# An MLP whose four engines follow one computed order, with seven-product groups in all but four places

## The chip, the cores and the metric

The kernel runs on one core of a Trainium2 chip. The metric is the device time of one execution in microseconds (us). Before the change three runs gave 2020.44 us in the median (2019.13 to 2021.89).

Five engines matter here: TensorE (PE in the profile; PEld is its weight load), VectorE (DVE), ScalarE (ACT), GpSimd (POOL, almost unused) and SyncE (SP), which issues the DMA transfers that bring weights from HBM. Each engine runs its own list of instructions in a fixed order and waits on semaphores.

## What is computed

A two-layer decoder trunk on 256 tokens of width 2048, in float32. Each layer is a mixer, a norm, an MLP and a norm; the change is in the MLP only:

```python
def sq_relu_mlp(x, w1, w2):
    return jnp.square(jax.nn.relu(x @ w1)) @ w2          # 2048 -> 8192 -> 2048

for layer in range(DEPTH):                                # DEPTH = 2
    mix = short_conv_mixer(...) if layer < N_A else mla_mixer(...)
    h = layer_norm(ALPHA * h + mix, ln_g[layer, 0], ln_b[layer, 0])
    h = layer_norm(ALPHA * h + sq_relu_mlp(h, mlp_w1[layer], mlp_w2[layer]), ln_g[layer, 1], ln_b[layer, 1])
```

## The kernel before

Every float32 weight is split into a high part `hi`, rounded to the format float32r by ScalarE (`split`, L144), and a rest `lo`, formed by VectorE (L145). A product x·w is then three matmuls, hi·w_hi, hi·w_lo, lo·w_hi (`dot`, L307 to L309), or two of 512 and 256 columns where the activations' two parts stand side by side (`mm_like`, L242 and L246). Weights stream through six raw buffers (`raw`, 512 KB each) into a ring of eight `hi`/`lo` pairs (`whl`, WA = 8).

The MLP has 64 chunks of 128 hidden units. The first eight come out of the fused norm; each of the other 56, a step "m" of the list `steps`, takes 16 matmuls of 512 columns and 16 of 256 into the bank `ps_m`, is moved out by ScalarE and VectorE (`whole`, L348 and L349) and squared. The second matrix is applied in 56 groups per layer: 28 pairs of chunks (j) by two halves (b) of the output. A group is a two-by-two block product. A "plain" group does it with eight products, into banks 1 to 4 of the accumulators `sum`. A "fast" group does it with seven (the Strassen-Winograd form) into seven banks: VectorE must first form four 512-wide differences of the weights (L193), and two more splits are due, `hi_t`/`lo_t` of 1024 and `t4` of 512. The last eight chunks go through `down` (`ps_d`) at the end.

Ten groups of a layer are plain (`PLAIN`, L39): j = 0 and 1 of both halves, and j = 4, 8, ..., 24 of the second half, where a run of that half begins. Since both halves share the banks, at each change of half ScalarE copies every bank to SBUF (`spill`, L595) and loads the other half's sum into it (`seed`, L599).

What runs when: `plan` lists groups and chunks in turn; the code emits each step's operations in that order, loads and splits running ahead by the ring; the language's scheduler then fixes each engine's list.

Of the kernel before, what the change touches and what calls it, by code (L numbers as in the profile page):

```python
# [15 lines left out]
P = 128  # L16
W = 256 + 2
# [19 lines left out]
SLOTS = 10  # L37
FIRST = ((0, 2, 4, 8), (0, 4, 8))
PLAIN = ((0, 1), (0, 1, *range(4, KEPT, 4)))  # L39
# [9 lines left out]
def trunk(ctx: ExitStack, tc: tile.TileContext, xT, vecs, w_in, w_out, w_kv, w_q, w_uk, w_uv,  # L49
          w_qn, w_qp, w_o, w1, w2, w2f, cosT, sinT, mask, ident, gb, out):  # L50
    nc = tc.nc
    PS = bass.MemoryType.PSUM
    const = ctx.enter_context(tc.tile_pool(name="const", bufs=1))
# [27 lines left out]
    def plan():  # L81

        nxt, b, steps, m, count = [0, 0], 0, [], QC, 0
# [10 lines left out]
        return steps + [("m", i) for i in range(m, FF // P)]  # L94

    steps = plan()

    def mlp_stream(l):
        out = halves(w1[l, :QC])
        for s in steps:  # L100
            if s[0] == "m":
                out += halves(w1[l, s[1]])
            else:
                out.append(("plain" if s[3] else "fast", w2f[l, s[1], s[2], 0], w2f[l, s[1], s[2], 1]))
        return out + halves(w2[l])

    stream += mlp_stream(0) + halves(w_kv) + halves(w_q)
# [3 lines left out]
    size = {"unit": 1, "plain": 2, "fast": 3}  # L111
# [27 lines left out]
    state = {"made": 0, "next": 0}  # L139
    ready = {}  # L140

    def split(hi, lo, src):

        nc.scalar.copy(hi, src)  # L144
        nc.vector.tensor_tensor(lo, src, hi.bitcast(F32), ALU.subtract)  # L145
# [7 lines left out]
    def load(i, raw, cuts):  # L153

        hi, lo = ready[i] = parts(i)
        for b0, b1 in zip(cuts, cuts[1:]):
            at, cols = slice(b0, b1), slice(P * b0, P * b1)
            nc.sync.dma_start(raw[:, cols], stream[i][1][:, cols])
# [4 lines left out]
    def load_raw(i, src):  # L163
        raw = raws.tile([P, 1024], F32, tag="raw", name=f"raw{i}")
        nc.sync.dma_start(raw, src)
        return raw

    def prepare(i):
# [15 lines left out]
        b11, b22, b21, b12 = r1[:, :BW], r1[:, BW:], r2[:, :BW], r2[:, BW:]  # L184
        out = {}
        if kind == "plain":
            out["11"], out["22"] = finished(r1, 1)
            yield
            out["21"], out["12"] = finished(r2, 2)
            ready[i] = out  # L190
            yield
            return
        minus = lambda o, x, y: nc.vector.tensor_tensor(o, x, y, ALU.subtract)  # L193
        out["11"], out["22"] = finished(r1, 1)
        minus(b11, b12, b11)
        minus(b12, b12, b22)
        minus(b22, b22, b11)
        yield
        out["T1"], out["T2"] = finished(r1, "t")
        minus(b11, b21, b22)  # L200
        yield
        out["21"], out["T3"] = finished(r2, 2)
        f = state["fast"].tile([P, 2, BW], F32R, tag="t4", name=f"t4_{i}", bufs=1)
        split(f[:, 0, :], f[:, 1, :], b11)
        out["T4"] = [f[:, 0, :], f[:, 1, :]]
# [3 lines left out]
    sequence, i = [], 2 * GROUP  # L209
    while i < len(stream):  # L210
        if [k for k, *_ in stream[i:i + 3]] == ["unit", "unit", "fast"]:
            sequence += [i + 2, i, i + 1, i + 2, i + 2]
            i += 3
        else:
            sequence += [i] * size[stream[i][0]]
            i += 1
# [12 lines left out]
    def take(n=2, ahead=None):  # L229
# [4 lines left out]
        make_up_to(max(mine, start[i] - 2 * GROUP + (WA if ahead is None else ahead)))  # L234
# [5 lines left out]
    def high(ps, w, blk, x, first):  # L240

        nc.tensor.matmul(ps, w[blk // 8][0][:, blk % 8, :], x, start=first, stop=False)  # L242

    def low(ps, w, blk, x, last):

        nc.tensor.matmul(ps[:, :T], w[blk // 8][1][:, blk % 8, :], x[:, :T], start=False, stop=last)  # L246
# [18 lines left out]
    def mm_k1(ps, w, blk, x, first, last):  # L265

        hi, lo = (t[:, blk % 8, :] for t in w[blk // 8])
        nc.tensor.matmul(ps[:, :T], lo, x[:, :T], start=first, stop=False)
        nc.tensor.matmul(ps[:, :T], hi, x[:, T:], start=False, stop=False)
        nc.tensor.matmul(ps[:, :T], hi, x[:, :T], start=False, stop=last)  # L270
# [6 lines left out]
    def mm_wide(wps, x, k0=0, k1=NC):  # L277

        for k in range(k0, k1):
            for w, ps in wps:  # L280
                hi, lo = (t[:, k % 8, :] for t in w[k // 8])
                nc.tensor.matmul(ps[:, :W], hi, x[k][:, :W], start=k == 0, stop=False)  # L282
                nc.tensor.matmul(ps[:, :W], lo, x[k][:, :W], start=False, stop=False)
                nc.tensor.matmul(ps[:, :W], hi, x[k][:, W:], start=False, stop=k == NC - 1)
# [20 lines left out]
    def dot(ps, w, x, first, last, goes_on=False):  # L305

        nc.tensor.matmul(ps, x[0], w[0], start=first, stop=False, skip_group_check=goes_on)  # L307
        nc.tensor.matmul(ps, x[0], w[1], start=False, stop=False, skip_group_check=goes_on)  # L308
        nc.tensor.matmul(ps, x[1], w[0], start=False, stop=last, skip_group_check=goes_on)  # L309
# [35 lines left out]
    def whole(ps, out):  # L345

        t = tmp.tile([P, T], F32, tag="evac", name="t")
        nc.scalar.copy(t, ps[:, T:])  # L348
        nc.vector.tensor_tensor(out, ps[:, :T], t, ALU.add)  # L349

    def put_split(dst, src):

        nc.scalar.copy(dst[:, :T], src)
# [787 lines left out]
```

## Time and profile before

| | |
|---|---|
| median of three runs | 2020.44 us |
| the profiled execution | 2019.17 us |
| its span, first to last instruction | 2017.4 us |
| groups and chunks of layer 1 | 412.78 to 1003.33 us |
| the same of layer 2 | 1363.19 to 1962.77 us |
| mean granted TensorE clock | 0.998 |

The two MLP stretches run from the first matmul into `sum` to the first into `ps_d`; together they are 59% of the span. In the views, a row of the timeline is start, duration, engine, line, operation, tiles and shape, with the idle time before it and what ended that in square brackets. A row of the groups gives count, busy time, mean duration in ns, then idle time and its releasers. A row of the windows gives for each engine the busy time in that stretch.

### The profile page before, as it was taken

How to read it: one execution, taken by the hardware profiler on the slowest of the kernel's cores; microseconds unless marked ns; L12 is line 12 of the kernel's file. 1: busy time of each engine (PE TensorE's matmuls, PEld its weight loads, DVE VectorE, ACT ScalarE, POOL GpSimd, SP SyncE). 2: the span in 40 equal slices, each digit the busy share in tenths (PEclk: the TensorE clock that was granted, in tenths of full speed). 3: DMA queues.
4: the chain of work that ended last, by engine and by line, in shares of the span. 5: the costliest groups of instructions: out<-in, count | busy, mean ns of one | idle time of the engine just before them, and what ended most of it. 6: DMA issues, size and time to landing. Idle time of an engine off the chain costs nothing.

```text
span 2017.4 us, 29774 instructions
## 1 busy us (share of the span) xinstructions
PE 1994.7 (99%) x11088; PEld 1737.5 (86%) x11088; DVE 1715.3 (85%) x2575; ACT 1381.1 (68%) x2071; POOL 2.3 (0%) x21
## 2 busy tenths in 40 slices
PE   9999999999999999999999999999999999999997
PEld 8888888988888888888889998898888888888886
DVE  7667677799999989999979878779999999898996
ACT  6444445587887788878756655568778788787871
POOL 0000000000000000000000000000000000000000
PEclk9999999999999999999999999999999999999999
DMA  9655556465666666666655534654666566565672
GB/s 321 205 188 189 189 188 193 149 184 186 194 209 188 211 206 188 211 187 219 228 176 165 162 119 136 195 176 151 206 197 210 176 209 202 180 219 184 209 236 99
DMA packets 108002, 385.31 MB, mean 191 GB/s; under 512 B 11984, under 2 KB 13392, under 8 KB 107856
## 3 DMA queue, kind: packets, MB, share of 16 engines
q1 hardware_dynamic: 107712, 383.13, 59.5%
q8 instruction: 87, 1.43, 0.3%
q14 instruction: 59, 0.48, 0.1%
q10 hardware_dynamic: 144, 0.26, 0.0%
HBM read 381.25 MB, written 2.10 MB: 190 GB/s over the span
## 4 chain that ended last, share of the span: by engine, by line
PE 82%; DVE 9%; ACT 4%; issue 2%; DMA 2%; DVEq 0%; ACTq 0%; SPq 0%
PE ps_m L242 16%; PE ps_u L242 13%; PE ps_m L246 8%; PE ps_u L246 7%; PE sum L307 7%; PE sum L308 7%; PE sum L309 7%; DVE lo L145 3%; DVE raw L193 2%; PE ps_d L309 1%; PE ps_d L308 1%; PE ps_d L307 1%; DMA raw<-in_w_dram 1%; ACT hi L144 1%; PE ps_w L282 1%
## 5 line engine op out<-in xcount | busy, mean ns | idle before, releaser
L145 DVE TENSOR_TENSOR lo<-raw,hi 128x1024 fp32r<-128x1024 f32 x712 | 856.3, 1219 | 126.5 <-ACT hi L144 49.3
L144 ACT CAST hi<-raw 128x1024 fp32r<-128x1024 f32 x712 | 735.4, 1052 | 273.5 <-PE ps_u L242 158.1
L242 PE MATMUL ps_m<-xhl,hi 128*128 128x512 f32 x1792 | 449.3, 391 | 2.3 <-DVE sf L349 2.1
L242 PEld LDWEIGHTS ps_m<-xhl,hi 128*128 128x128 f32 x1792 | 328.4, 188 | 68.2 <-DVE sf L349 3.9
L246 PEld LDWEIGHTS ps_m<-xhl,lo 128*128 128x128 f32 x1792 | 245.2, 190 | 17.9
L246 PE MATMUL ps_m<-xhl,lo 128*128 128x256 f32 x1792 | 250.8, 282 | 0.0
L307 PE MATMUL sum<-hi,hc 128*128 128x512 f32 x512 | 202.0, 395 | 4.8 <-ACT sum L599 4.8
L308 PE MATMUL sum<-lo,hc 128*128 128x512 f32 x512 | 200.4, 391 | 0.0
L193 DVE TENSOR_TENSOR raw<-raw,raw 128x512 f32<-128x512 f32 x276 | 189.0, 685 | 1.3
L309 PE MATMUL sum<-hi,ha 128*128 128x512 f32 x448 | 173.9, 390 | 0.0
L242 PE MATMUL ps_u<-xhl_a,hi 128*128 128x512 f32 x720 | 171.9, 391 | 0.0
L145 DVE TENSOR_TENSOR lo_t<-raw,hi_t 128x1024 fp32r<-128x1024 f32 x92 | 112.6, 1224 | 63.4 <-ACT hi_t L144 63.4
L242 PEld LDWEIGHTS ps_u<-xhl_a,hi 128*128 128x128 f32 x720 | 132.4, 188 | 25.7
L595 ACT COPY sums<-sum 128x512 f32<-128x512 f32 x204 | 118.4, 587 | 32.6 <-PE sum L309 31.9
L144 ACT CAST hi_t<-raw 128x1024 fp32r<-128x1024 f32 x92 | 96.6, 1050 | 56.1 <-DVE raw L193 55.5
L307 PEld LDWEIGHTS sum<-hi,hc 128*128 128x128 f32 x512 | 96.4, 188 | 27.7 <-ACT sum L599 10.2
L599 ACT COPY sum<-sums 128x512 f32<-128x512 f32 x186 | 110.9, 596 | 1.3
L308 PEld LDWEIGHTS sum<-lo,hc 128*128 128x128 f32 x512 | 96.5, 188 | 16.2
L348 ACT COPY t<-ps_m 128x256 f32<-128x256 f32 x112 | 41.7, 372 | 89.1 <-PE ps_m L246 89.1
L309 PEld LDWEIGHTS sum<-hi,ha 128*128 128x128 f32 x448 | 84.2, 188 | 17.6
L246 PEld LDWEIGHTS ps_u<-xhl_a,lo 128*128 128x128 f32 x720 | 92.3, 191 | 3.5
L246 PE MATMUL ps_u<-xhl_a,lo 128*128 128x256 f32 x720 | 93.4, 283 | 0.0
(240 smaller groups left out, 3273.9 us busy)
## 6 DMA issues: line engine op xcount, KB each, us to landing
raw<-in_w_dram SPq DMA_DIRECT2D x288, 512.0 KB, 4.4
raw<-in_w2f_dram SPq DMA_DIRECT2D x224, 512.0 KB, 4.1
raw<-in_w_in_dram SPq DMA_DIRECT2D x90, 512.0 KB, 4.3
raw<-in_w_out_dram SPq DMA_DIRECT2D x32, 512.0 KB, 4.0
raw<-in_w_o_dram SPq DMA_DIRECT2D x32, 512.0 KB, 3.7
raw<-in_w_kv_dram SPq DMA_DIRECT2D x10, 512.0 KB, 4.0
raw<-in_w_q_dram SPq DMA_DIRECT2D x8, 512.0 KB, 3.8
raw<-in_w_uk_dram SPq DMA_DIRECT2D x8, 512.0 KB, 4.4
```

The costliest lines, as they stand in the source:

```text
L144: nc.scalar.copy(hi, src)
L145: nc.vector.tensor_tensor(lo, src, hi.bitcast(F32), ALU.subtract)
L193: minus = lambda o, x, y: nc.vector.tensor_tensor(o, x, y, ALU.subtract)
L242: nc.tensor.matmul(ps, w[blk // 8][0][:, blk % 8, :], x, start=first, stop=False)
L246: nc.tensor.matmul(ps[:, :T], w[blk // 8][1][:, blk % 8, :], x[:, :T], start=False, stop=last)
L282: nc.tensor.matmul(ps[:, :W], hi, x[k][:, :W], start=k == 0, stop=False)
L307: nc.tensor.matmul(ps, x[0], w[0], start=first, stop=False, skip_group_check=goes_on)
L308: nc.tensor.matmul(ps, x[0], w[1], start=False, stop=False, skip_group_check=goes_on)
L309: nc.tensor.matmul(ps, x[1], w[0], start=False, stop=last, skip_group_check=goes_on)
L348: nc.scalar.copy(t, ps[:, T:])
L595: nc.scalar.copy(self.slot(self.live.pop(p)), self.bank[p])
L599: nc.scalar.copy(self.bank[p], self.at(key))
```

## The change

Three things change. First, `PLAIN` becomes 2: only j = 0 and 1 of each half are plain, so 52 groups of a layer are fast instead of 46. Second, the loop over `steps` in `mlp` is replaced by a list of all operations of the stage (class `Work`): each has its engine (T, A, V for TensorE, ScalarE, VectorE; S for a load), a length worked out from its columns, what it depends on, and a function that issues it. `times` gives every VectorE and ScalarE operation a latest start by which TensorE would not wait; `arrange` plays the engines against each other from these lengths, always taking the ready operation with the earliest such time; `issue` emits all in the order of their starts, and `keep_in_program_order` holds every engine, and SP's queue of loads, to it. The first four groups (`ALONE`) are loaded as before, ahead of the stage. Third, small things go along: an eleventh slot for spilled sums, T4 before T3 within a fast group, `prepare` of the next norm as operations of the list, the mask loaded in the attention part instead of at the start, and the weights of `down` requested after all loads of the list (`stops`). Since all operations go through a wrapper, they stand under L70 in lists of the changed kernel.

```diff
-SLOTS = 10
-PLAIN = ((0, 1), (0, 1, *range(4, KEPT, 4)))
+SLOTS = 11
+SPARE = 2
+ALONE = 4
+LEAD = 9000
+PLAIN = 2
...
+            def call(*args, **named):
+                ins = op(*args, **named)
+                kept = state["kept"]
+                if kept is None:
+                    return ins
+                if self not in kept:
+                    kept.add(self)
+                    return ins
+                return tc.keep_in_program_order(ins)
...
-            run = [(b, j, j in PLAIN[b]) for j in range(nxt[b], end)]
-            for i, (b, j, plain) in enumerate(run):
-                steps.append(("group", b, j, plain, i == 0, i == len(run) - 1))
-                if count >= 3 and m < FF // P:
-                    steps.append(("m", m))
-                    m += 1
-                count += 1
+            groups += [(b, j, j < PLAIN, j == end - 1) for j in range(nxt[b], end)]
...
+    def mlp_stream(l):
+        return halves(w1[l, :QC]) + [("plain", w2f[l, b, j, 0], w2f[l, b, j, 1]) for b, j, *_ in groups[:ALONE]]
...
+        stops.append(len(stream))
+        return halves(w2[l])
...
-        if [k for k, *_ in stream[i:i + 3]] == ["unit", "unit", "fast"]:
-            sequence += [i + 2, i, i + 1, i + 2, i + 2]
...
+            if stops and i >= stops[0]:
+                return
...
+        LATER = {"A": 140, "V": 125, "T": 210}
...
+            late, t = [0.0] * n, 0.0
+            for i, op in enumerate(self.ops):
+                if op[0] == "T":
+                    late[i] = t
+                    t += op[1]
+            for i in reversed(order):
+                engine, cost, _, _, early = self.ops[i]
+                if engine in "AV":
+                    late[i] = min([late[u] - (cost + self.LATER[engine] if ends else 0) for u, ends in self.users[i]],
+                                  default=t) - early
+            return late
...
+                    begun[i] = max(now, queue)
+                    queue = begun[i] + 100
+                    pipe = max(pipe, begun[i] + 1700) + 1550
+                    heapq.heappush(events, (pipe + 1000, i))
+                for e in "TAV":
+                    while free[e] <= now:
+                        if e == "T":
+                            if not turn or turn[0] not in able:
+                                break
+                            i = turn.pop(0)
+                        elif ready[e]:
+                            i = heapq.heappop(ready[e])[1]
+                        else:
+                            break
+                        begun[i], free[e] = now, now + ops[i][1]
+                        heapq.heappush(events, (free[e], -1))
+                        heapq.heappush(events, (free[e] + self.LATER[e], i))
+                        settle(i, False)
...
+            order = self.arrange(freed)
+            self.room = [None] * RAW
+            state["kept"] = set()
+            for i in order:
+                if self.ops[i][0] == "S" and self.room[self.places[i]] is None:
+                    self.room[self.places[i]] = raws.tile([P, 1024], F32, tag="raw", name=f"w{i}")
+                self.ops[i][2]()
+            state["kept"] = None
...
+        spans = {"A": lambda n: 0.82 * n + 110, "V": lambda n: n / 0.96 + 68}
...
+            ends.append(work.add("T", count * (columns + 32) / 2.4, run, known(deps), ends[-1:]))
...
+            c = add("A", 1024, lambda: scalar.copy(both()[0], raw()), load, *deps)
+            return both, c, add("V", 1024, lambda: less(both()[1], raw(), both()[0].bitcast(F32)), c)
...
+                first = ring_ops(loads[0])
+                x1 = add("V", BW, lambda: less(b11(), b12(), b11()), first[2], loads[1])
+                x3 = add("V", BW, lambda: less(b12(), b12(), b22()), x1)
+                x2 = add("V", BW, lambda: less(b22(), b22(), b11()), x3)
+                mid, end = ring_ops(loads[0], x2), ring_ops(loads[1], x3)
+                x4 = add("V", BW, lambda: less(b11(), b21(), b22()), mid[2])
...
+                x = add("A", BW, fourth, x4, fourths[-1])
+                l4 = add("V", BW, lambda: less(box["f"][:, 1, :], b11(), box["f"][:, 0, :].bitcast(F32)), x)
...
+                x = add("A", 512, lambda: sums.spill(p), banked[p], behind=back[-SPARE:-SPARE + 1 or None])
...
+                x = add("A", 512, lambda: sums.seed(p, key), x)
...
+        for i in range(ALONE):
+            group_ops(i)
+        made, loads = chunk_ops(QC)
+        work.loads += loads
+        entries += [c for _, c, _ in made]
+        for m, i in enumerate(range(ALONE, len(groups)), QC + 1):
+            made, loads = chunk_ops(m)
+            more, others = group_ops(i)
+            work.loads += [*others, *loads]
+            entries += [more[0][1], made[0][1], more[1][1], made[1][1], more[2][1]]
...
+                work.ops[e][3].append((frees[entries[n - WA]], True))
+                if not isinstance(entries[n - 1], tuple):
+                    work.ops[e][3].append((entries[n - 1], False))
+        work.issue(freed)
+        stops.pop(0)
```

VectorE in layer 1, before: the end of the fast group (0, 5) of half 0 (tiles `raw165`), the plain group (1, 4) of half 1 (`raw168`), and the start of the next fast group. `lo166` and `lo167` are the splits of a chunk, `sf` is a chunk being moved out.

```order
L193 TENSOR_TENSOR raw165_0_4762<-raw165_0_4762 128x512 [waits DVE_49]
L349 TENSOR_TENSOR sf_4818<-ps_m_4785,t_4819 128x256 [waits Activation_49]
L145 TENSOR_TENSOR lo165_t_4823<-raw165_0_4762,hi165_t_4822 128x1024 [waits Activation_49]
L145 TENSOR_TENSOR lo165_2_4828<-raw165_1_4764,hi165_2_4827 128x1024 [waits Activation_49]
L193 TENSOR_TENSOR raw165_0_4762<-raw165_1_4764,raw165_0_4762 128x512 [waits DVE_49]
L145 TENSOR_TENSOR lo166_4859<-raw166_4856,hi166_4858 128x1024 [waits DMAHW3_49,PE_49,Activation_49]
L145 TENSOR_TENSOR lo167_4865<-raw167_4862,hi167_4864 128x1024 [waits DMAHW4_49,PE_49,Activation_49]
L145 TENSOR_TENSOR t4_165_4831<-raw165_0_4762,t4_165_4831 128x512 [waits PE_49,Activation_49]
L145 TENSOR_TENSOR lo168_1_4873<-raw168_0_4868,hi168_1_4872 128x1024 [waits DMAHW5_49]
L349 TENSOR_TENSOR sf_4818<-ps_m_4876,t_4909 128x256 [waits Activation_49]
L145 TENSOR_TENSOR lo168_2_4955<-raw168_1_4870,hi168_2_4954 128x1024 [waits DMAHW6_49]
L145 TENSOR_TENSOR lo171_1_4963<-raw171_0_4958,hi171_1_4962 128x1024 [waits DMAHW7_49,Activation_49]
```

The plain group has only its two splits, `lo168_1` and `lo168_2`. In the fast group `lo165_t` stands two rows behind the difference that it splits (first row), with one short operation between.

VectorE in the same place now; the group (1, 4) is fast, its weights are in `w108` and `w107`, and its three splits are the ring's `lo1_0`, `lo1_2` and `lo1_4`. `lo1_1` and `lo1_3` are splits of a chunk.

```order
L70 TENSOR_TENSOR lo1_0_4237<-w108_4185,hi1_0_4236 128x1024 [waits DMAHW4_49,Activation_49]
L70 TENSOR_TENSOR t4_4881<-w76_4179,t4_4881 128x512 [waits Activation_49]
L70 TENSOR_TENSOR w108_4185<-w107_4183,w108_4185 128x512 [waits DMAHW5_49,DVE_49]
L70 TENSOR_TENSOR sf_4906<-ps_m_4847,t_4898 128x256 [waits Activation_49]
L70 TENSOR_TENSOR w107_4183<-w107_4183,w108_4185 128x512 [waits DVE_49]
L70 TENSOR_TENSOR lo1_1_4291<-w88_4187,hi1_1_4290 128x1024 [waits DMAHW6_49]
L70 TENSOR_TENSOR w108_4185<-w108_4185 128x512 [waits DVE_49]
L70 TENSOR_TENSOR ha1_4152<-sf_4738,hc1_3515 128x1024
L70 TENSOR_TENSOR lo1_2_4325<-w108_4185,hi1_2_4324 128x1024 [waits Activation_49]
L70 TENSOR_TENSOR lo1_3_4335<-w89_4189,hi1_3_4334 128x1024 [waits DMAHW7_49,PE_49,Activation_49]
L70 TENSOR_TENSOR w108_4185<-w107_4183,w108_4185 128x512 [waits DVE_49]
L70 TENSOR_TENSOR lo1_4_4393<-w107_4183,hi1_4_4392 128x1024 [waits Activation_49]
```

Four differences have been added (the rows that write `w108` or `w107`) and a third split; the split of the fourth difference (`t4_4979`) is two rows further on. Between the third difference and its split `lo1_2` there stands now a 1024-wide operation of a chunk (`ha1`).

More of the change, by code (lines that the diff above doesn't have):

```diff
@@ L227, in make_up_to, with take @@
             next(making[i])
[L229 removed]
+    def take(n=2):
         i = state["next"]
@@ L718, in parts_of @@
             return dict(zip(NAMES, both))
[L720 removed]
+        layer, sums = idx // 2, Sums(idx)
         Banks.only = Banks.more
[L722 to L748 removed]
@@ new lines, in mlp, with add, product @@
+        if after is not None:
+            after.prepare(0)
+        work, freed, ring, place, entries, frees = Work(), {}, {}, {}, [], {}
+        spans = {"A": lambda n: 0.82 * n + 110, "V": lambda n: n / 0.96 + 68}
+        known = lambda deps: [d for d in deps if d is not None]
+        def add(engine, n, run, *deps, behind=(), early=0):
+            return work.add(engine, spans[engine](n), run, known(deps), behind, early)
+        ends = []
+        def product(columns, count, run, *deps):
+            ends.append(work.add("T", count * (columns + 32) / 2.4, run, known(deps), ends[-1:]))
+            return ends[-1]
```

613 lines of the change are left out of this document (385 added, 228 removed).

## The prediction

> **What bounds the kernel now.** I read the page's first lines and its chain of waits first.
>
> ```profile
> span 2017.4 us, 29774 instructions
> PE 1994.7 (99%) x11088; PEld 1737.5 (86%) x11088; DVE 1715.3 (85%) x2575; ACT 1381.1 (68%) x2071; POOL 2.3 (0%) x21
> PE 82%; DVE 9%; ACT 4%; issue 2%; DMA 2%; DVEq 0%; ACTq 0%; SPq 0%
> ```
>
> TensorE is busy almost throughout and carries the chain, but VectorE has 9% of it. The change lies in the two MLP stretches, so the windows come next: one row per stretch with busy time on PE, PEld, DVE and ACT.
>
> ```profile
> 412.78:1003.33 590.55, 588.86 (x3003) 501.27 (x3002) 545.67 (x722) 470.80 (x676) 0.00 (x0) 1.00 0.63 199
> 1363.19:1962.77 599.58, 593.73 (x3033) 502.75 (x3031) 546.52 (x710) 473.51 (x676) 0.00 (x0) 1.00 0.62 198
> ```
>
> VectorE stands at 92% and 91% there, second to TensorE. A busy TensorE need not run at its pace, since a matmul that is held up counts as busy for a while; so the timeline gives the pace, start to start.
>
> ```profile
> 561.98 0.39 PE L307 MATMUL sum<-t,hc 128*128 128x512 f32 x1
> 562.21 0.39 PE L308 MATMUL sum<-t,hc 128*128 128x512 f32 x1
> 562.43 0.39 PE L309 MATMUL sum<-t,ha 128*128 128x512 f32 x1
> 562.66 1.98 PE L242 MATMUL ps_m<-xhl,hi 128*128 128x512 f32 x8
> 564.47 1.12 PE L246 MATMUL ps_m<-xhl,lo 128*128 128x256 f32 x8
> 565.43 0.86 PE L242 MATMUL ps_m<-xhl,hi 128*128 128x512 f32 x3
> ```
>
> Three matmuls of 512 columns take 0.68 us (561.98 to 562.66), so one takes 0.2267; eight of 256 take 0.96, one 0.12. A stretch has 56 chunks of 16 and 16 matmuls, 56 × 16 × 0.3467 = 310.6 us, and 10 × 8 + 46 × 7 = 402 products of three, 402 × 0.68 = 273.4: together 584.0. Layer 1 took 590.55, so 6.6 us were lost. In layer 2 some transposes of the residual stand inside the stretch:
>
> ```profile
> 1936.80 0.60 PE L1017 MATMUL turned<-id_t,xres 128*128 128x128 f32 x4
> 1937.33 0.97 PE L242 MATMUL ps_m<-xhl,hi 128*128 128x512 f32 x3
> 1959.79 3.22 PE L1017 MATMUL turned<-id_t,xres 128*128 128x128 f32 x28
> 1962.77 0.48 PE L307 MATMUL ps_d<-hi,hc 128*128 128x512 f32 x1
> ```
>
> They take 0.5 + 3.0 = 3.5 us, so layer 2 lost 599.58 − 584.0 − 3.5 = 12.1. What TensorE's weight loads (PEld, ahead of each matmul) waited for says where: total, times and longest in us, the first two rows layer 1, the next two layer 2, then the largest single case.
>
> ```profile
> PEld ps_m L242 <- DVE sf L349: 2.5, 2, 2.0
> PEld sum L307 <- ACT sum L599: 2.1, 6, 0.5
> PEld sum L307 <- ACT sum L599: 10.7, 19, 2.3
> PEld ps_m L242 <- DVE sf L349: 1.4, 3, 1.0
> 1709.28 0.39 PE L307 MATMUL sum<-hi,hc 128*128 128x512 f32 x1
> 1710.89 0.59 ACT L599 COPY sum<-sums 128x512 f32<-128x512 f32 x1
> 1711.54 0.50 PE L307 MATMUL sum<-hi,hc 128*128 128x512 f32 x1 [1.87 <-ACT sum L599]
> ```
>
> At a change of half a bank is reloaded too late (L599), and now and then the one bank of the chunks is emptied too late (L349). No row has TensorE waiting for a split of weights on VectorE: VectorE is not the bound now.
>
> **The change part by part.** *Fewer products.* Six groups per layer lose one product: 12 × 0.68 = 8.2 us off the engine that bounds. Both stretches then need 396 × 0.68 + 310.6 = 579.9 us.
>
> *More VectorE work.* The forms of a fast group in layer 1, and how closely such operations follow each other:
>
> ```profile
> L193 DVE TENSOR_TENSOR raw<-raw,raw 128x512 f32<-128x512 f32 x138 | 94.4, 684 | 0.4
> L193 DVE TENSOR_TENSOR raw<-raw 128x512 f32<-128x512 f32 x46 | 31.4, 682 | 0.0
> L145 DVE TENSOR_TENSOR lo_t<-raw,hi_t 128x1024 fp32r<-128x1024 f32 x46 | 56.3, 1224 | 32.0 <-ACT hi_t L144 32.0
> L145 DVE TENSOR_TENSOR t<-raw,t 128x512 fp32r<-128x512 f32 x46 | 31.5, 684 | 0.4 <-ACT t L144 0.4
> 711.12 0.68 DVE L193 TENSOR_TENSOR raw<-raw,raw 128x512 f32<-128x512 f32 x1
> 711.72 2.35 DVE L145 TENSOR_TENSOR lo<-raw,hi 128x1024 fp32r<-128x1024 f32 x2
> 713.99 0.68 DVE L145 TENSOR_TENSOR t<-raw,t 128x512 fp32r<-128x512 f32 x1
> 714.60 0.68 DVE L193 TENSOR_TENSOR raw<-raw,raw 128x512 f32<-128x512 f32 x1
> ```
>
> A 512-wide operation holds VectorE 0.60 us (711.12 to 711.72), a 1024-wide one 1.135 (711.72 to 713.99, two). A converted group adds four differences, a `lo_t` and a `t4` split: 4 × 0.60 + 1.135 + 0.61 = 4.15 us, six of them 24.9 us per layer. VectorE's work goes from 545.7 to 570.6 us in layer 1 and from 546.5 to 571.4 in layer 2, while TensorE needs 579.9: still less, but with only 9 us to spare where 45 us stood idle. This hides behind TensorE as long as VectorE hardly waits; without that cover it costs up to its full 24.9 per layer (both ends are kept for the range). [...]
>
> *ScalarE.* Six casts of 1024 and six of 512 come, and six spills and six seeds go, per layer:
>
> ```profile
> L144 ACT CAST hi_t<-raw 128x1024 fp32r<-128x1024 f32 x46 | 48.3, 1050 | 15.8 <-DVE raw L193 15.7
> L144 ACT CAST t<-raw 128x512 fp32r<-128x512 f32 x46 | 28.6, 621 | 0.0
> L595 ACT COPY sums<-sum 128x512 f32<-128x512 f32 x102 | 59.1, 586 | 28.4 <-PE sum L309 28.2
> L599 ACT COPY sum<-sums 128x512 f32<-128x512 f32 x93 | 55.4, 595 | 0.5
> ```
>
> That is 6 × (1.05 + 0.62) − 12 × 0.59 = +2.9 us on an engine with 120 us free per stretch: nothing, hidden by TensorE; uncovered it would cost these 2.9 us per layer.
>
> *The computed order.* It ranks a seed or the emptying of a bank ahead of casts that have time, which speaks to the waits quoted above: 2.1 + 10.7 = 12.8 us for seeds and 2.5 + 1.4 = 3.9 for the chunks' bank. From above it can win the 6.6 + 12.1 = 18.7 us lost; from below nothing, or it adds the waits of the second rival. Which of its own waits remain no trace of before shows. The nearest row is layer 1, where the same copies at the same changes of half made TensorE wait 2.1 us and not 10.7: an order can do that much better in one layer, but both layers now have less room on VectorE. I take half of the seeds' 12.8 and a third of the 3.9 as won: 6.4 + 1.3 = 7.7 us.
>
> The converted groups also stand at changes of half: before, every second change led into a plain group, now all lead into fast ones, which need seven banks and not four. That is ScalarE's work already counted, but it comes in bursts; I keep the other half of the 12.8 us as the price of it.
>
> *Loads.* The same weights are loaded, in as many transfers:
>
> ```profile
> raw<-in_w2f_dram SPq DMA_DIRECT2D x224, 512.0 KB, 4.1
> mask_t<-in_mask_dram SPq DMA_DIRECT2D x1, 192.0 KB, 4.9
> ```
>
> SP's queue now holds the planned order. Two things in it could block: a fast group keeps both its raw buffers until `t4` is split, and everything queued behind waits with it, which is the same as in the 46 fast groups of before; and the mask, moved behind the loads for `down`, waits for memory of the MLP that is free by then and is first needed in attention. The loads of `down` come last in the list, with up to eight ring entries of lead. All at nothing: the DMA engines are busy 0.63 of the stretch; if the cover went, a late weight would cost TensorE up to 4.1 us.
>
> **Sum.** 8.2 + 7.7 = 15.9; span 2017.4 − 15.9 = 2001.5 us. The profiled execution was 2019.17, 1.8 above its span, and the median of the runs is 1.3 above that one. Forecast: 2004.5 us in the median, own range 1997 to 2011.
>
> **Rivals.**
>
> *Products only.* The order wins nothing back, because the waits at the changes of half come from the burst of some 14 copies on ScalarE, which remains. For it: 195 copies in layer 1 become 183 by the counts above, hardly fewer. Against it: layer 1's 2.1 us with the same copies. 2020.4 − 8.2 = 2012.3 us.
>
> *VectorE becomes the bound; slower.* Place: the dependent chain difference, cast on ScalarE, split on VectorE, in the fast groups. If a strict order leaves VectorE waiting as before, its time sets the pace. It idled 590.55 − 545.67 = 44.9 us in layer 1 and 53.1 in layer 2. If the `lo_t` waits halve (32.0 to 16) and the rest stays, layer 1 takes 570.6 + 28.9 = 599.5 and layer 2, with the row below, 571.4 + 37.4 = 608.8: 18 us more, 2038.6 us; with all idle time kept, 2070 us. It decides from 590.55 − 570.6 = 20 us of idle time in layer 1.
>
> ```profile
> DVE lo_t L145 <- ACT hi_t L144: 31.4, 36, 1.2
> ```
>
> Against it: idle time of an engine that runs ahead is slack and not need, and TensorE never waited for a split. The Trainium skill (Perfetto Trace Analysis, Identifying the Most-Contended Engine) takes occupancy as a fair measure for VectorE and not for TensorE; by it VectorE, at 571 of 580 us, would be the most contended engine, which is this rival's case.
>
> *Not what it says.* The order holds the products' gain but loses it again at the start of each stretch, where the first chunk needs all of the normalised inputs: 2016.4 to 2024.5, no change.
>
> **How the numbers follow.** Forecast 0.62, products only 0.14, no change 0.08, VectorE as bound 0.16. What can be told from no change on this kernel is 0.2%, 4 us; so faster 0.76, same 0.08, slower 0.16. No time below 1993.5 is possible by these terms (8.2 + 18.7 less than now); the range that leaves out 2 in 10 is 1997 to 2019.
>
> **What would show it.** Right: 18 fewer matmuls into `sum` in each stretch (1188 for 1206); layer 1 in 584 to 588 us and layer 2 in 588 to 594; VectorE busy near 570 in both; seeds at half or less of their 12.8 us among TensorE's waits; less idle time ahead of the middle split. Wrong: TensorE waiting for splits (`lo` or `t4`) by more than 3 us per stretch, VectorE above 97% of a stretch that is longer than 591 us, seeds at their old total, or a gap where a stretch or `down` begins.

## The result, and the profile after

The changed kernel took 2009.47 us in the median of four runs (2008.3 to 2010.63); the kernel before, four times beside it, 2021.16 (2019.13 to 2023.75): a ratio of 0.9941, interval 0.9924 to 0.9959. The profiled execution took 2008.99 us.

From the page after, the span and the busy time of the engines:

```profile
span 2007.2 us, 29664 instructions
PE 1985.3 (99%) x11052; PEld 1735.7 (86%) x11052; DVE 1762.7 (88%) x2647; ACT 1392.4 (69%) x2071; POOL 2.3 (0%) x21
```

The two stretches in the view by windows (span of the window, its length, then PE, PEld, DVE, ACT and POOL, granted clock, DMA share, GB/s):

```profile
412.92:1003.56 590.64, 585.96 (x2982) 500.43 (x2981) 570.39 (x758) 477.81 (x676) 0.00 (x0) 0.99 0.63 199
1363.50:1951.97 588.47, 587.11 (x3015) 501.70 (x3013) 566.27 (x744) 477.01 (x675) 0.00 (x0) 1.00 0.64 198
```

TensorE has 36 matmuls fewer than before (11052 for 11088), 18 per layer as forecast. VectorE's work in layer 1 rose as computed (570.39 us, 570.6 expected); in layer 2 it is 566.27, 5.1 below the 571.4 expected. Yet layer 1 gained nothing (590.55 before), and layer 2 gained all of it, 11.1 us. The waits of TensorE's weight loads, first layer 1, then layer 2, and what VectorE waited for ahead of its splits in the two layers (total, times and longest in us):

```profile
PEld ps_m L70 <- ACT sums L70: 4.7, 1, 4.7
PEld sum L70 <- ACT sum L70: 0.6, 1, 0.6
...
PEld ps_m L70 <- DVE sf L70: 1.1, 1, 1.1
PEld sum L70 <- ACT sum L70: 0.7, 1, 0.7
...
DVE lo L70 <- ACT hi L70: 10.4, 16, 1.3
DVE lo L70 <- ACT hi L70: 14.0, 19, 1.7
```

The seeds' waits fell from 12.8 to 1.3 us (0.6 + 0.7), and VectorE's waits for the casts ahead of all its splits of weights to 10.4 and 14.0 us, from 32.0 and 31.4 ahead of the middle splits alone. One new wait stands in layer 1, once, 4.7 us long: a chunk's bank `ps_m` that waits for a copy into `sums`. The timelines of ScalarE and TensorE there, put together, some rows left out:

```profile
978.45 1.06 ACT L70 CAST hi<-w 128x1024 fp32r<-128x1024 f32 x1 [1.89 <-DMA w<-in_w_dram]
979.60 0.39 PE L70 MATMUL sum<-hi,ha 128*128 128x512 f32 x1
981.36 1.04 ACT L70 CAST hi<-w 128x1024 fp32r<-128x1024 f32 x1 [1.85 <-DMA w<-in_w_dram]
982.72 1.04 ACT L70 CAST hi<-w 128x1024 fp32r<-128x1024 f32 x1 [0.32 <-DMA w<-in_w_dram]
983.67 0.58 ACT L70 COPY sums<-sum 128x512 f32<-128x512 f32 x1
984.30 3.78 PE L70 MATMUL ps_m<-xhl,hi 128*128 128x512 f32 x8 [4.31 <-ACT sums L70]
```

The copy that empties the bank (983.67) stands behind three casts that wait for loads. TensorE starts the next chunk 4.70 us after the last product instead of 0.23. And its eight matmuls last until 987.88, 3.58 us instead of 1.81, since the granted clock (third column from the right) is halved after the pause:

```profile
979.00:984.00 5.00, 0.99 (x5) 0.49 (x3) 5.00 (x6) 2.83 (x4) 0.00 (x0) 0.88 0.91 329
984.00:988.00 4.00, 3.70 (x9) 2.92 (x10) 4.00 (x5) 2.24 (x3) 0.00 (x0) 0.50 0.86 297
988.00:992.00 4.00, 4.00 (x22) 3.65 (x21) 1.29 (x2) 1.36 (x2) 0.00 (x0) 0.80 0.97 372
```

### The profile page after: what moved, and what is told of

Same layout as the page of the kernel before. It is cut to its first block, busy times and chain, and to the rows that moved or that the text cites. A ratio compares the mean times of both kernels' runs of the same rounds, so it can differ in the third digit from the quotient of the medians.

```text
span 2007.2 us, 29664 instructions
## 1 busy us (share of the span) xinstructions
PE 1985.3 (99%) x11052; PEld 1735.7 (86%) x11052; DVE 1762.7 (88%) x2647; ACT 1392.4 (69%) x2071; POOL 2.3 (0%) x21
## 4 chain that ended last, share of the span: by engine, by line
PE 86%; DVE 8%; ACT 3%; issue 2%; DMA 1%; DVEq 0%; ACTq 0%
PE ps_m L70 25%; PE sum L70 21%; PE ps_u L70 21%; PE ps_d L70 4%; PE ps_w L70 4%; DVE lo L70 4%; PE ps_g L70 3%; DVE w L70 2%; ACT hi L70 1%; PE ps_q L70 1%; PE ps_v L70 1%; PE S L70 1%; PE ps_k L70 1%; PE ps_wo L70 1%; ACT sums L70 1%
## 5 line engine op out<-in xcount | busy, mean ns | idle before, releaser
L70 DVE TENSOR_TENSOR lo<-w,hi 128x1024 fp32r<-128x1024 f32 x536 | 638.6, 1219 | 27.4 <-ACT hi L70 24.5
L70 ACT CAST hi<-w 128x1024 fp32r<-128x1024 f32 x536 | 531.4, 1054 | 143.7 <-DVE w L70 131.1
L70 ACT CAST hi<-raw 128x1024 fp32r<-128x1024 f32 x280 | 291.6, 1051 | 257.1 <-PE ps_u L70 158.1
L70 PE MATMUL ps_m<-xhl,hi 128*128 128x512 f32 x1792 | 448.2, 392 | 5.5 <-ACT sums L70 4.3
L70 DVE TENSOR_TENSOR lo<-raw,hi 128x1024 fp32r<-128x1024 f32 x280 | 335.9, 1221 | 116.3 <-ACT hi L70 40.1
L70 PEld LDWEIGHTS ps_m<-xhl,hi 128*128 128x128 f32 x1792 | 330.0, 189 | 70.4 <-ACT sums L70 4.7
L70 PE MATMUL sum<-hi,hc 128*128 128x512 f32 x736 | 278.0, 391 | 0.5 <-ACT sum L70 0.5
L70 PEld LDWEIGHTS ps_m<-xhl,lo 128*128 128x128 f32 x1792 | 245.2, 191 | 18.2 <-DVE lo L70 0.7
L70 PE MATMUL sum<-lo,hc 128*128 128x512 f32 x656 | 256.5, 391 | 0.0
L70 PE MATMUL ps_m<-xhl,lo 128*128 128x256 f32 x1792 | 250.8, 283 | 0.0
L70 PE MATMUL sum<-hi,ha 128*128 128x512 f32 x640 | 246.5, 389 | 0.0
L70 DVE TENSOR_TENSOR w<-w,w 128x512 f32<-128x512 f32 x312 | 213.1, 683 | 0.7
L70 PE MATMUL ps_u<-xhl_a,hi 128*128 128x512 f32 x720 | 172.0, 391 | 0.0
L70 PEld LDWEIGHTS sum<-hi,hc 128*128 128x128 f32 x736 | 138.6, 188 | 27.1 <-ACT sum L70 1.3
L70 PEld LDWEIGHTS ps_u<-xhl_a,hi 128*128 128x128 f32 x720 | 132.4, 188 | 25.7
L70 PEld LDWEIGHTS sum<-hi,ha 128*128 128x128 f32 x640 | 120.2, 188 | 25.9
L70 PEld LDWEIGHTS sum<-lo,hc 128*128 128x128 f32 x656 | 123.6, 188 | 21.6
L70 ACT COPY sums<-sum 128x512 f32<-128x512 f32 x194 | 109.6, 597 | 13.4 <-PE sum L70 12.8
L70 ACT COPY sum<-sums 128x512 f32<-128x512 f32 x174 | 104.2, 610 | 0.8
L70 PEld LDWEIGHTS ps_u<-xhl_a,lo 128*128 128x128 f32 x720 | 92.3, 191 | 3.5
L70 ACT ACTIVATE sf<-sf 128x512 f32<-128x512 f32 x120 | 76.6, 639 | 26.8 <-DVE sf L70 25.7
L70 PE MATMUL ps_w<-xd,hi 128*128 128x258 f32 x512 | 94.4, 284 | 0.5 <-DVE xres L70 0.5
```

The source lines that it names most:

```text
L70: ins = op(*args, **named)
```

## The experiments

The ratio is to the kernel before, run beside each on the same chip; the stretches, in us, are from one profiled execution each. The kernel before took 2019.99 to 2021.37 us in these comparisons, so that small differences between rows are better read from the ratios.

| run | median us | ratio, interval | layer 1 | layer 2 |
|---|---|---|---|---|
| changed kernel | 2009.47 | 0.9941 [0.9924, 0.9959] | 590.6 | 588.5 |
| chunk keeps its bank (tail_bank) | 2003.79 | 0.9912 [0.9898, 0.9925] | 583.6 | 588.4 |
| that bank in both layers (tail_both) | 2013.42 | 0.9960 [0.9946, 0.9973] | 590.9 | 593.0 |
| ten plain groups, computed order (order_ten) | 2008.54 | 0.9934 [0.9922, 0.9947] | 586.4 | 591.6 |
| four plain groups, order of before (products) | 2114.40 | 1.0464 [1.0450, 1.0478] | 642.8 | 642.2 |
| + 17.4 us VectorE work (vec_load) | 2035.23 | 1.0073 [1.0058, 1.0089] | 601.3 | 603.5 |
| + 34.8 us (vec_load2) | 2066.87 | 1.0230 [1.0215, 1.0245] | 617.6 | 619.4 |
| − 31.2 us (less_diff) | 2000.96 | 0.9905 [0.9888, 0.9921] | 582.9 | 587.8 |
| order emitted, not held (not_held) | 2001.40 | 0.9905 [0.9889, 0.9922] | 583.3 | 588.1 |
| the same, chunk keeps its bank (not_held_tail) | 2002.39 | 0.9914 [0.9899, 0.9929] | 583.2 | 589.2 |
| products, middle cast first (products_late) | 2213.46 | 1.0953 [1.0937, 1.0970] | 690.1 | 690.8 |
| products, splits pinned (products_held) | 2119.90 | 1.0490 [1.0473, 1.0507] | 645.0 | 646.1 |
| due times ignored (by_index) | 2156.75 | 1.0678 [1.0660, 1.0696] | 661.4 | 664.9 |

**The one new wait.** Chunk 61 is the first of three that may take any bank. In layer 1 it falls on the bank of `sum1`; in layer 2 it keeps the chunks' own. The plan names the emptying of `sum1` as a condition for chunks 62 and 63 only. The first run lets the choice begin one chunk later, the second makes chunk 61 take a bank of the sums in both layers.

```diff
-                    if m >= FF // P - 3:
+                    if m >= FF // P - 2:
                         Banks.only = None
```

> The changed kernel, but the third chunk from the end keeps the chunks' own bank; only the last two take a bank of the sums. Theory: what layer 1 gave away is one wait near its end, where this chunk takes the bank of sum 1, which ScalarE empties only behind casts that wait for loads; TensorE stands for 4.5 us and then runs at a granted clock of 0.50 for some 4 us, 7.8 us together. Then this kernel takes 2009.5 - 7.8 = 2001.7 us, layer 1 some 583 us, and no clock below 1.00 there. Rival: loads and splits are late at this place anyway, so the wait goes to the next chunk's weights: 2006 us or more, layer 1 at 587 or more.

```diff
-                        Banks.only = None
+                        Banks.only = pmm if m == FF // P - 3 else None
```

> The changed kernel, but in both layers the third chunk from the end takes a bank of the sums (in the changed kernel only layer 1 does so). Theory: the same wait appears in layer 2, 4 to 5 us and a drop of the clock after it: 2009.5 + 7.8 = 2017 us, layer 2 some 596 us. Rival (something else of layer 1, such as the next norm's operations, makes VectorE and ScalarE late): layer 2 stays at 588.5 us, total 2009.5.

The windows of the first of the two runs:

```profile
415.02:998.62 583.60, 583.23 (x2982) 498.35 (x2981) 567.29 (x755) 477.83 (x676) 0.00 (x0) 1.00 0.65 200
1358.51:1946.92 588.41, 587.08 (x3014) 501.66 (x3013) 566.44 (x744) 476.52 (x675) 0.00 (x0) 1.00 0.64 198
```

Layer 1 lost 7.04 us (590.64 − 583.60) to this one bank, layer 2 changed by 0.06. The medians differ by less, 5.7 us; the profiled execution with the bank kept was about 2 us late before the stretch began (75 matmuls in its first 20 us, 86 in the changed kernel's), ahead of all that differs. Forced into layer 2, the same pause came there, 4.18 us of idle time before 1934.54, with the clock at 0.58 behind it, and the stretch grew by 4.6 us:

```profile
1934.54 3.69 PE L70 MATMUL ps_m<-xhl,hi 128*128 128x512 f32 x8 [4.18 <-ACT sums L70]
...
1934.00:1938.00 4.00, 3.46 (x8) 2.78 (x9) 4.00 (x5) 2.48 (x4) 0.00 (x0) 0.58 0.99 344
```

So the cause is shown by removing it and by making it anew; its price depends on place, 7.0 and 4.6 us.

**The two halves of the change.** The order with the ten plain groups of before (and chunk 61 on its own bank), and the four plain groups in the order of before:

```diff
-            groups += [(b, j, j < PLAIN, j == end - 1) for j in range(nxt[b], end)]
+            groups += [(b, j, j < PLAIN or b == 1 and j % 4 == 0, j == end - 1) for j in range(nxt[b], end)]
...
```

> The computed order with the ten plain groups of before (and the bank of the run tail_bank). Theory: order and products add up, so this is 8.2 us above the run tail_bank, some 2010 us, each stretch some 4.1 us longer, and VectorE idle 20 to 45 us in each. Rival: the order's gain needs the fast groups, since plain groups in the list bring waits of their own at the changes of half: 2014 us or more. Other rival: VectorE limits the all-fast kernel, so giving it 24.9 us less work per layer costs less than 8.2 us: 2006 us or less.

```diff
-PLAIN = ((0, 1), (0, 1, *range(4, KEPT, 4)))
+PLAIN = ((0, 1), (0, 1))
```

> The kernel before with its old order, and 52 groups by seven products instead of 46. Theory of the forecast: 8.2 us less TensorE work and 24.9 us more VectorE work per layer, which the old order does not hide fully; 2011 to 2018 us, most likely 2014, VectorE near 570 us in each stretch. Rival, products only: 2012.3 to 2013. Rival, VectorE becomes the bound where its waits stay: slower than before, 2025 to 2040 us, VectorE's idle time in a stretch still above 20 us.

The windows of the first:

```profile
412.64:999.04 586.40, 586.40 (x3000) 501.92 (x2999) 545.30 (x719) 472.65 (x675) 0.00 (x0) 1.00 0.63 198
1359.13:1950.77 591.64, 590.14 (x3032) 505.12 (x3031) 545.10 (x709) 472.35 (x675) 0.00 (x0) 1.00 0.61 197
```

Against before, the order, with the small things that go along with it, wins 4.15 and 7.94 us in the stretches, 12.1 together (12.8 in the medians, 2021.37 for the kernel before in that comparison). What the small things are worth apart was not tried. The products, added in the computed order, win 2.80 and 3.23, 6.0 of the 8.2 us (4.75 in the medians; in the profiled execution with fewer products the first stretch began 2.4 us later, ahead of all that differs). In the order of before they cost 93 us; the three expectations, 2011 to 2040 us between them, all missed. The windows of that run, and what VectorE and then TensorE's weight loads waited for in layer 1:

```profile
413.25:1056.03 642.78, 603.47 (x2985) 504.32 (x2984) 571.83 (x759) 480.02 (x676) 0.00 (x0) 0.98 0.57 185
1415.81:2058.00 642.19, 604.57 (x3014) 506.02 (x3013) 568.34 (x746) 479.96 (x676) 0.00 (x0) 0.98 0.57 185
```

```profile
DVE lo_t L145 <- ACT hi_t L144: 51.3, 47, 2.8
DVE sf L676 <- ACT sf L669: 15.1, 11, 1.7
...
PEld ps_m L242 <- DVE sf L349: 51.0, 31, 2.7
```

VectorE has the work of the changed kernel and idles 71 us beside it, 643 us together in layer 1; TensorE meets its lateness at the chunks' bank. The timeline of one such place (DVE and PE rows):

```profile
743.97 1.22 DVE L145 TENSOR_TENSOR lo<-raw,hi 128x1024 fp32r<-128x1024 f32 x1
745.11 0.69 DVE L193 TENSOR_TENSOR raw<-raw 128x512 f32<-128x512 f32 x1
745.71 0.42 DVE L349 TENSOR_TENSOR sf<-ps_m,t 128x256 f32<-128x256 f32 x1
746.18 2.75 PE L242 MATMUL ps_m<-xhl,hi 128*128 128x512 f32 x8 [2.32 <-DVE sf L349]
746.90 1.23 DVE L145 TENSOR_TENSOR lo_t<-raw,hi_t 128x1024 fp32r<-128x1024 f32 x1 [0.78 <-ACT hi_t L144]
```

VectorE does not pause before `sf`: it works off splits of weights for later, late itself, while the bank that TensorE needs waits behind them. Then it stands idle for the cast whose difference it formed two operations before. This is the place that the rival "VectorE becomes the bound" names, and the run is dearer than its 2070 us: the idle time did not stay at 45 us but grew to 71. Whether the chain at that place is what makes the order late is tried further down.

**How much room VectorE has.** All with the computed order and chunk 61 on its own bank. Each fast group gets one or two more operations of 256 columns ahead of the split of T4, or loses its fourth difference (that kernel's products take an unformed block instead, so it does not compute the MLP).

```diff
-                l4 = add("V", BW, lambda: less(box["f"][:, 1, :], b11(), box["f"][:, 0, :].bitcast(F32)), x)
+
+                def extra():
+                    s = tmp.tile([P, T], F32, tag="sq", name="extra")
+                    vector.tensor_tensor(s, cos_t, sin_t, ALU.add)
+
+                e = x4
+                e = add("V", T, extra, e)
+                l4 = add("V", BW, lambda: less(box["f"][:, 1, :], b11(), box["f"][:, 0, :].bitcast(F32)), x, e)
```

> The changed kernel with the chunks' own bank kept to the end (2003.79 us), and in each of the 52 fast groups of a layer one more VectorE operation of 256 columns, whose result nobody reads (nothing of the output changes). One such operation holds VectorE 0.34 us, so 52 of them are 17.4 us per layer: VectorE's work goes from 567.3 to 584.7 us in layer 1 and from 566.4 to 583.8 in layer 2, where TensorE needs 579.9. Theory one (VectorE's idle time of now, 16.3 and 22.0 us, is slack): it is used up first, the stretches take what VectorE needs and some 3 us, 588 and 592 us, 2010 to 2014 in all. Theory two (the idle time is needed by the chains from difference to cast to split, as the rival of the prediction had it): the stretches grow by the whole 17.4 us each, to 601 and 606, 2038.6 in all.

> The same with two such operations in each fast group: 34.8 us more VectorE work per layer, 602.1 us in layer 1 and 601.2 in layer 2, clearly over TensorE's 579.9. Theory one (idle time is slack, VectorE's work alone counts): stretches of 605 and 608 us, 2044 to 2050 in all. Theory two (idle time is needed): 618 and 623 us, 2073 in all. Should the planned order fail altogether once VectorE bounds, as it may since its due times come from TensorE alone, the stretches go beyond 630 us.

```diff
-                x4 = add("V", BW, lambda: less(b11(), b21(), b22()), mid[2])
+                x4 = mid[2]
```

> The changed kernel with the chunks' own bank kept to the end (2003.79 us), with the fourth difference of each fast group left out: its products take an unformed block of the weights, and VectorE has 52 x 0.60 = 31.2 us less work per layer, 536 of the 567 us. Theory one (VectorE's work plus some 16 to 22 us of idle time that it cannot avoid, 583.6 and 588.4 us, is what ends the stretches): they fall until TensorE bounds, to its 579.9 us and the remainder that the run with ten plain groups had, 582.3 and 587.5 us, about 2001.5 in all, and no further, however much work went. Theory two (something else takes the 3.7 us above 579.9): 583.6 and 588.4 us stay, 2003 to 2005. Should VectorE have held up more than the stretches tell, 1999 or less.

The windows of the first and of the third of these:

```profile
414.54:1015.79 601.25, 594.08 (x2983) 500.79 (x2981) 582.83 (x808) 475.93 (x676) 0.00 (x0) 1.00 0.65 194
1375.66:1979.16 603.50, 596.70 (x3014) 503.79 (x3013) 580.34 (x796) 476.24 (x677) 0.00 (x0) 1.00 0.64 193
```

```profile
413.68:996.62 582.94, 582.61 (x2982) 498.33 (x2981) 538.66 (x704) 477.02 (x676) 0.00 (x0) 1.00 0.63 200
1356.42:1944.22 587.80, 586.35 (x3014) 501.57 (x3013) 538.78 (x694) 477.69 (x677) 0.00 (x0) 1.00 0.63 199
```

More work lengthens the stretches by almost all of it, near theory two: 17.7 and 15.1 us for 17.4, 34.0 and 31.0 for 34.8. (By the profile VectorE's busy time grew a little less than planned, by 15.5 and 13.9 us and by 33.0 and 32.3; the run with less work lost 28.6 and 27.7 of the planned 31.2.) Less work shortens them by 0.7 and 0.6, to within 0.7 us of what theory one gave there. The kernel stands at the knee, within about 1 us. Above the knee VectorE's idle time in layer 1 stays at 16 to 18 us (583.60 − 567.29, 601.25 − 582.83): needed, as theory two had it; in layer 2 it is 21 to 23. Below, it is slack: 582.94 − 538.66 = 44.3 us cost nothing. The added operation always stands ahead of the split of T4; other places were not tried. Of the 2.2 us that the fewer products lack in the stretches, VectorE explains at most 1.3 (0.7 + 0.6); the rest is open.

**Is it the holding?** The wrapper returns each instruction as it is, and the language's scheduler may move it.

```diff
-                return tc.keep_in_program_order(ins)
+                return ins
```

> The changed kernel (2009.47 us) with the computed order emitted as before, but no engine held to it: the language's scheduler may again move operations. Theory one (the emission in computed order does the work): 2006 to 2013 us, seeds' waits still under 3 us per layer. Theory two (it is the holding): the scheduler moves casts and splits back towards the old places, the waits of seeds and of the chunks' bank return in part, 2016 us or more.

> The computed order emitted but not held (2001.4 us), and the chunks' own bank kept to the end as well, which won 5.7 us where the order was held. Theory one (the bank hurts only because the held order puts its emptying behind casts that wait for loads; unheld, the copy runs ahead of them): nothing left to win, 1999.5 to 2003.5 us. Theory two (taking that bank costs by itself): 5 us less, 1996 to 1998.

Both theories of the first missed: 8.1 us less than the changed kernel in the medians, 7.3 by the ratios. ScalarE's timeline at chunk 61 of layer 1, not held:

```profile
976.50 0.58 ACT L70 COPY sums<-sum 128x512 f32<-128x512 f32 x1
976.97 1.05 ACT L70 CAST hi<-w 128x1024 fp32r<-128x1024 f32 x1
979.60 1.05 ACT L70 CAST hi<-w 128x1024 fp32r<-128x1024 f32 x1 [1.58 <-DMA w<-in_w_dram]
```

The scheduler put the copy ahead of the casts, though the plan does not name it for this chunk. With the bank kept as well (edited as in the first diff) nothing more was won, as theory one of the second run had it. So holding each engine to the order won nothing here; it only made a mistake of the plan binding. Between 2001.40 and 2003.79 us lie 0.07% by the ratios, less than their intervals.

**What in the order does it.** Two tries mended the order of before with the four plain groups at its dependent chain alone. One put the middle cast right behind the third difference and its split two splits later; the other pinned the casts and splits of the chunks and of the middle, so that the chunks' splits stand between that difference and its split; ScalarE's order was to stay almost the same.

```diff
...
-        out["T1"], out["T2"] = finished(r1, "t")
+        th, tl = parts(f"{i}_t")
+        nc.scalar.copy(th, tiled(r1))
+        yield
+        nc.vector.tensor_tensor(tl, tiled(r1), th.bitcast(F32), ALU.subtract)
...
-            sequence += [i + 2, i, i + 1, i + 2, i + 2]
+            sequence += [i + 2, i + 2, i, i + 1, i + 2, i + 2]
...
```

> The kernel before with the fewer plain groups (2114.4 us), and one edit: in a fast group the middle cast comes right behind the third difference, and its split on VectorE comes two splits of a chunk later, not next but one; the work is the same. The ring runs ahead by nine steps instead of eight, since a fast group now counts four steps. Theory one (the chain difference, cast, split makes VectorE wait, and VectorE's time with those waits sets the pace): the waits of the middle split, 51.3 and 52.2 us, fall below 15 each; the stretches fall from 642 to about 600 us each, 2025 to 2040 in all. Theory two (VectorE's operations are too many and in a wrong order, so that the chunks' bank is emptied late; the waits are only a sign of it): the time stays above 2090 us, and VectorE waits elsewhere.

```diff
+    def pinned(ins):
+        return tc.keep_in_program_order(ins) if state.get("mlp") else ins
...
-            split(hi, lo, tiled(raw))
+            split(hi, lo, tiled(raw), pinned)
...
-            split(*w, tiled(r))
+            split(*w, tiled(r), pinned if name == "t" else lambda ins: ins)
...
```

> The kernel before with the fewer plain groups (2114.4 us), and the casts and splits of the chunks' weights and of the middle of a fast group pinned to the order in which the code emits them: on VectorE two splits of 1024 columns now stand between the third difference and the split of it, where one operation of 256 or none stood; ScalarE's order stays almost the same, the work is the same. Theory one (VectorE waits out each cast because its split stands right behind the difference, and these waits push VectorE's time over TensorE's): the waits of the middle split, 51.3 and 52.2 us, fall below 20; stretches of about 607 us instead of 642, 2030 to 2060 in all. Theory two (the waits move to other splits, as when the middle cast was put first, since ScalarE's own list is what runs late): VectorE's idle time stays near 70 us per stretch and the time above 2090 us.

Waits in layer 1 of the first, of TensorE's weight loads and of VectorE, and of the second, of VectorE and of ScalarE:

```profile
PEld sum L311 <- ACT hi_t L200: 76.2, 44, 2.8
PEld ps_m L246 <- ACT hi L144: 30.9, 46, 1.4
...
DVE lo L145 <- ACT hi L144: 100.4, 52, 3.8
```

```profile
DVE ha L145 <- ACT hc L144: 37.7, 24, 2.9
DVE t L145 <- ACT t L144: 14.9, 19, 2.4
DVE lo_t L145 <- ACT hi_t L144: 7.5, 12, 0.7
...
ACT hi L144 <- DMA raw<-in_w_dram: 54.4, 35, 4.1
```

The first try was 99 us slower than the order it was to mend: TensorE now waits 76.2 us for the middle cast itself, and VectorE 100.4 for the casts of chunks. The pins took the middle split's waits from 51.3 to 7.5 us, and not a microsecond off the time: VectorE now waits for other casts, and ScalarE 54.4 us for loads (3.3 without the pins). So theory one fell in both: taking that one wait away saves nothing. But each try brought waits of its own, so they do not show what makes the old order late; that stays open. The last run plays the engines against each other as the computed order does, and takes only the rank away:

```diff
-                    heapq.heappush(ready[engine], (late[i], i))
+                    heapq.heappush(ready[engine], (i, i))
```

> The changed kernel with the chunks' own bank kept to the end (2003.79 us), its order computed in the same play of the engines, but of several ready operations the one that stands first in the list is taken (the place at which the program adds it), not the one with the earliest latest start. Same work, same holding. Theory one (the due times do it, by ranking a seed or the emptying of a bank ahead of casts that have time): the waits of seeds and of the chunks' bank return to about the 16.7 us that the kernel before had, or more since VectorE has nothing to spare: 2015 us or more. Theory two (the play itself does it: an operation is placed only when it is ready by the plan, so that none waits at the head of its engine's list): waits under 5 us per layer, 2002 to 2008 us. In the kernel before with the same products, whose order has neither, the time was 2114.4 us.

Its waits in layer 1, of TensorE's weight loads, of VectorE and of ScalarE:

```profile
PEld ps_m L70 <- ACT hi L70: 54.2, 39, 2.9
DVE lo L70 <- ACT hi L70: 68.9, 43, 3.1
...
ACT hi L70 <- DVE w L70: 100.9, 29, 6.9
```

It is 153 us slower than with the due times: this order lives by its rank, against the one other rank that was tried. The time is that of theory one (2015 us or more), but not its mechanism: it is not the seeds that come late but the casts of the chunks (54.2 us), while VectorE waits 68.9 us for ScalarE's casts and ScalarE 100.9 for VectorE's differences (10.4 and 65.5 in the changed kernel). How much of this each engine's rank carries was not tried.

## Why the prediction was right or wrong

*What bounds.* Right: TensorE, with VectorE second, but far closer than forecast. With chunk 61 on its own bank, 31.2 us less VectorE work win 0.7 us in layer 1, and 17.4 us more cost 17.7.

*Fewer products, 8.2 us.* The sign is right, the term too large: 6.0 us in the stretches, 4.75 in the medians. And it holds only with the computed order. The step that hid their VectorE work, "still less, but with only 9 us to spare", was mis-sized: 579.9 − 570.6 compared work with work, but VectorE also needs some 17 us of waits for casts, so that there was about nothing to spare. That explains at most 1.3 us of what lacks. The rival "VectorE becomes the bound" set its point at 20 us of idle time in layer 1. What VectorE needed there at its bound was 16 to 18, just short of it. The rule of the Trainium skill (Perfetto Trace Analysis, Identifying the Most-Contended Engine) that VectorE's occupancy is a fair measure was nearer than the forecast on this side: 17.4 us more work cost 17.7.

*ScalarE and the loads, at nothing.* ScalarE's work hid (477.8 us in a stretch of 590.6), though it grew by 7.0 and 3.5 us where 2.9 was worked out. The loads did for all but one place: there casts late by their loads held up a copy, and TensorE stood for 4.31 us, near the 4.1 given as the price "if the cover went". That is chance: three casts waited in a row (1.89, 1.85 and 0.32 us), and with the lower clock behind the pause the price was 7.0. The prediction looked for such blocking in SP's queue, not in ScalarE's.

*The computed order, 7.7 us.* Too small: 12.8 us in the medians, with the small things that go along. The seeds' waits fell to a tenth and not to half; the bursts at changes of half, for which half was kept back, cost 1.3 us of waits in this order. What was missed is that the plan may be wrong on one bank: no term of the sum has that. The sum came out at 11.9 us (ratio) for 15.9 because 12.8 + 4.75 − 5.7 (the bank) stand for 7.7 + 8.2; one error partly cancelled two others. So it is in part luck that the time lies in the range of 1997 to 2011 us, 5 us above the forecast: a loss that no term foresaw met a gain that was taken too small.

*By stretch.* Layer 2 came as forecast (588.5 of 588 to 594). Layer 1 did not: 590.6 instead of 584 to 588, all through chunk 61; with its bank kept it takes 583.6. None of the signs named for wrong came, but VectorE's share was close: 96.6% of 590.6 us, where 97% of more than 591 was the mark.

*Rivals.* "Products only" is out: the order wins 12.8 us with the ten plain groups, and the products without it cost 93. Its 2012.3 us lie only 2.8 from the measured time, so it is these runs that decide, not the time. "VectorE becomes the bound" did not come about in the changed kernel, but 17.4 us more work brings it. "Not what it says" is out: the stretches begin where they did (412.92 us for 412.78, and the second 359.94 us behind the end of the first for 359.86).

The fastest kernels here that compute the whole MLP are the computed order not held, 2001.40 us (2002.39 with chunk 61 on its own bank), and held with that bank kept, 2003.79.

## What to carry to other kernels

An engine's room is not the other engine's time less its work: some of its idle time is needed by dependent chains. Add a known bit of work and look whether the time follows; that finds the knee directly. Where two engines feed each other, the place where a wait shows need not be what makes it: taking away the waits of one split moved them elsewhere and saved nothing. A plan that fixes an order must know every resource that the code will really take, or leave the last word to a scheduler that sees it.

## What the hardware showed that was not expected

A pause of TensorE can cost more than its length, and not always. The granted clock after three pauses of similar length, around the one of 2.3 us in the run with the four plain groups in the order of before:

```profile
744.00:746.00 2.00, 0.00 (x0) 0.00 (x0) 2.00 (x4) 0.18 (x1) 0.00 (x0) 1.00 0.81 246
746.00:748.00 2.00, 1.82 (x7) 1.50 (x8) 1.22 (x2) 2.00 (x3) 0.00 (x0) 0.85 0.95 358
748.00:750.00 2.00, 2.00 (x9) 1.81 (x8) 2.00 (x4) 1.98 (x3) 0.00 (x0) 0.50 0.27 111
750.00:752.00 2.00, 2.00 (x9) 1.71 (x9) 2.00 (x2) 1.30 (x2) 0.00 (x0) 0.79 0.52 123
```

and around one of 2.4 us in the run with pinned splits, where it stayed at 1.00, as it did after the 1.9 us of before:

```profile
739.00:741.00 2.00, 0.00 (x0) 0.00 (x0) 1.56 (x2) 2.00 (x5) 0.00 (x0) 1.00 0.00 0
741.00:743.00 2.00, 1.48 (x5) 0.96 (x6) 1.71 (x2) 2.00 (x3) 0.00 (x0) 1.00 0.00 0
```

If the clock is halved while it is low, the first took (0.15 + 0.50 + 0.21) × 2 / 0.5 = 3.4 us of half clock, and the changed kernel's pause (0.12 × 5 + 0.50 × 4 + 0.20 × 4) / 0.5 = 6.8, twice as much. The pause forced into layer 2, 4.18 us for 4.31, took only 0.42 × 4 / 0.5 = 3.4. At half clock half of the time is lost, so this makes 1.7 us of the difference between the two prices of that pause, 7.0 and 4.6 us. The Trainium skill (TensorE: Matmul & The Clock Gate, Part 1: The HAM clock gate) tells of half rate after an idle window of about 3.4 us that runs freely. The lengths agree with that window; that 2.3 us of idle time were enough does not.
